# One matrix per chunk in the RWKV-7 chain, the sample's squares at rows 12 and 22, and the dense work in another order

## The chip, the core and the metric

The program runs on one NeuronCore of a Trainium2 chip. The metric is the device time of one execution in microseconds (us), taken as the median of several executions. TensorE (PE) does the matrix products, VectorE (DVE), ScalarE (ACT) and GpSimd (POOL) the elementwise work, and SyncE (SP) issues all the DMAs.

## What is computed

Two layers of a hybrid decoder for a prompt of 512 tokens and a sample group of 8 times 4 tokens (544 columns in all). Layer 0 is windowed attention, layer 1 is RWKV-7 time mixing; both also attend to 256 memory tokens. The change is almost wholly in layer 1, whose core is this recurrence over a state S of 64x64 for each of 12 heads:

```python
def step(S, inp):
    r_t, w_t, k_t, v_t, a_t, b_t = inp
    sa = jnp.einsum('bhvk,bhk->bhv', S, a_t)
    S = S * w_t[:, :, None, :] + sa[..., None] * b_t[:, :, None, :] + v_t[..., None] * k_t[:, :, None, :]
    return S, jnp.einsum('bhvk,bhk->bhv', S, r_t)
...
p = xn @ w_in                                  # 29 column tiles of 128: r, k, v, LoRA, memory query, gate
y = group_norm(y) + sum(r * k * r_k) * v
h = concat([y, o_mem]) * silu(gate)
return h @ w_out
```

## The kernel before

**Layout.** Activations stand as features on partitions and tokens along the free axis. Dense products with weights are split in a high and a low part (`mm1`, L309): three matmuls of 128x128 by 272 or 256 columns (fp32r) for each tile of 128 inputs. Everything else on PE is fp32 and stands in the trace as two records for each matmul that the code issues: the 32 matmuls of a round of 64x64 blocks are 64 records.

**The chunked recurrence.** The 512 prompt tokens are 8 chunks of 64. The 12 heads are three groups g of four heads (two pairs j, each with two heads h). For each pair `decay`, `keys`, `receptance`, `values` and `scores` (L1224 to L1396) prepare the chunk products: `SA` holds the masked scores against a, `SR` those against r, `UV` values and a by token, `BK` the keys by token, and `st.DF` the decay over each whole chunk. `products(g)` (L1400) inverts a 64x64 triangle for each chunk and head: 30 steps of two dependent DVE operations over PSUM (L1444 and L1446), then two rounds of 32x32 products (X, L1460 and L1469). In the steps s = 5 and s = 12 it also squares the sample's small matrix (`square`, L1427). Then come three rounds of 64x64 products: w (L1480, into `AR`), q (the scores times the values) and v (the inverse times q, both L1495), q and v in place in `UV[:, 0]`.

**The chain.** `recur(g)` (L1615) goes through the 8 chunks. In each chunk PE multiplies the state by w (z, four matmuls), DVE adds u (L1670), PE multiplies by the keys (z again, four or eight matmuls), DVE adds the decayed state (L1688), which POOL made (Sd, L1672). The outputs y are products put between these steps (`y_of`, L1635), normalised in `norm` after 4 chunks (`YB`; group 2 in portions of 4, 2 and 2). The next group's inversion cannot begin before `end{g}`: T, the inversion's PSUM tile, and z, the chain's, share one buffer of two banks ("zs"). All groups thus follow one another: inversion, products, chain, inversion, ...

**The order of the work.** `Flow` (L172) is a small planner written by hand: streams (generators) yield a cost and a latency, and the one with the lowest rank that is ready is emitted next; dense streams (`dense` with the column products, `gates`, `outer`) fill in between by a debt rule (`RHO`, `DEBT`). `LAT` are the planned latencies, `RANK` the ranks. The instruction order that results is then ordered on each engine by the framework's own list scheduler; at run time every engine works strictly in that order.

**Around the end.** `gates` (L1736) makes 8 gate columns in the order `GORDER`, the first `GEARLY` without waiting for the last column. They go to DRAM (`ud`). `outer` (L1809) then reads them back (`gated`, L1749: DMA, DVE, ACT, POOL for each of six tiles), into `h1`, which takes the memory of the projections' input `xg` and so cannot be written before the last gate's matmuls. The output projection ("o1", six of eight input tiles, 288 matmuls) follows, and `last` (L1769) for each half of the tokens: the last two tiles (4 and 5) once group 2's norm is done, then the norm and the residual.

**Layer 0.** The sample's cached keys and values come through a ring of `CCB` tiles of 512 KB (`cc`, L654); `sample_values` (L847) reads nine of them for each half of the sample.

Of the kernel before, what the change touches and what calls it, by code (L numbers as in the profile page):

```python
# [24 lines left out]
GORDER = (6, 7, 0, 1, 2, 3, 4, 5)  # L25
# [203 lines left out]
def _device(tc, I, O):  # L229
# [853 lines left out]
    ind2 = rw.tile([128, 2], F32, name="ind2")  # L1083
    hv = rw.tile([128, 4, 6], F32, name="hv")
# [139 lines left out]
    def decay(p):  # L1224
# [30 lines left out]
        for h, r in enumerate(H2):  # L1255
            nc.gpsimd.tensor_copy(st.DF[r, h ^ j], R_[r, 63:512:64])
# [60 lines left out]
    def scores(p):  # L1317
# [74 lines left out]
        yield from by_token((AR.rearrange("p j x t -> p (j x t)"), 2 * j * NT), (q.xv, 0), lambda x: UV[:, x, j], st.UVs[:, j], "av")  # L1392
# [5 lines left out]
    Q0, Q1 = [slice(64 * hh, 64 * hh + 32) for hh in range(2)], [slice(64 * hh + 32, 64 * hh + 64) for hh in range(2)]  # L1398

    def products(g):  # L1400
# [40 lines left out]
        for s in range(1, 31):  # L1441
# [31 lines left out]
        yield f"tokens{2 * g + 1}"  # L1473
        for e in range(2):
            pt = ps_t(f"w{g}{e}")
            for j in range(2):
                for i in range(4):
                    for c, h in block(i, j, e):
                        a = (4 * j + i) * 64
                        nc.tensor.matmul(pt[H2[h], a:a + 64], UV[unit(c, j, h)[0], 0, j, unit(c, j, h)[1]],  # L1480
                                         SA[unit(c, j, h)[0], 0, j, score(c, j, h)[1]], start=True, stop=True)
            both[e](AR[:, :, 0, 0:512].rearrange("p j (i e t) -> p j i e t", e=2, t=64)[:, :, :, e],
                    pt.rearrange("p (j i t) -> p j i t", j=2, t=64))
            yield 1.0, 0

        u = st.u = UV[:, 0].rearrange("p j (c e v) -> p (j c) e v", c=4, e=2)
        for k in range(2):
            for i in range(2):
                pt = ps_t(f"{'qv'[k]}{g}{i}")
                for c in range(4 * i, 4 * i + 4):  # L1490
                    for j, h in PAIRS:
                        r, cs = score(c, j, h)
                        e = turned(c, j, h)
                        a = (c % 4 * 2 + e) * 64
                        nc.tensor.matmul(pt[r, a:a + 64], SA[r, 1 - k, j, cs],  # L1495
                                         u[r, c, e] if k else UV[r, 1, j, unit(c, j, h)[1]], start=True, stop=True)
                both[i](UV[:, 0, i], pt)
                yield 1.0, 0
# [116 lines left out]
    def recur(g):  # L1615

        st = sts[g]
# [3 lines left out]
        AR, BK, SR, UV, DF, u = st.AR, st.BK, st.SR, st.UV, st.DF, st.u  # L1621
        St = rw.tile([128, 2, 64], F32, tag="St", bufs=4, name=f"St{g}i")
        nc.vector.memset(St, 0.0)
        zs = ps_zs(f"z{g}").rearrange("p (e k c v) -> p e k c v", k=2, c=4, v=64)
        yps = None

        states, last = [], None

        def put(out, lhs, rhs, start, stop):
            nc.tensor.matmul(out, lhs, rhs, start=start, stop=stop)  # L1630
            if last:
                tc.add_manual_dep(flow.last(), last.name, SYNC, reason="one half of a bank")
            tc.stamp_issue_order_token(flow.last(), f"chain{g}")

        def y_of(cs, e):  # L1635


            nonlocal yps
            a, b = [ab for ab in YB[g] if ab[0] <= cs[0] < ab[1]][0]
            if cs[0] == a and e:  # L1640
                yps = ps_c("y", f"y{g}_{a}")
            steps = [(c, k, t) for c in cs for k in range(3) for t in range(2) if (c or k) and (k == 0 and t) == e]
            for step in steps:
                c, k, t = step
                for j, h in PAIRS:
                    if turned(c, j, h) == t:
                        r, s = score(c, j, h)
                        lhs = SR[r, 2 - k, j, s] if k else AR[H2[h], j, 1, CH[c]]
                        rhs = (UV[r, 1, j, unit(c, j, h)[1]] if k == 1 else u[r, c, t] if k else states[c][H2[h], j ^ h])
                        y = ((c - a) * 2 + h) * 64  # L1650
                        put(yps[r, y:y + 64], lhs, rhs, e and step == steps[0], not e and step == steps[-1])
            c = cs[1]
            if e:
                return
            if c == b - 1:
                def out(pt):
                    pt = pt[:, 0:(b - a) * 128].rearrange("p (c j t) -> p c j t", j=2, t=64)
                    for j in range(2):
                        add_affine(2 * g + j, pt[:, :, j], slice(64 * a, 64 * b), True)
# [149 lines left out]
    def outer():  # L1809
        for e in ("gates", "end1", "norm1_8", "norm1s"):  # L1810
            yield e
# [125 lines left out]
```

## Time and profile before

| | |
|---|---|
| median of 3 runs | 826.03 us (824.16 to 829.28) |
| the profiled execution | 825.58 us, of which its span is 823.8 us |
| mean granted TensorE clock | 0.956 of full speed |
| PE busy | 759.0 us (92%) |
| DVE busy | 457.7 us (56%) |
| POOL busy | 353.0 us (43%) |
| ACT busy | 339.4 us (41%) |

The span is what the profile shows; 1.8 us of the execution lie around it. A busy PE is not PE at its peak: a matmul's end is modelled, and at the lower granted clock (1.2 in place of 2.4 GHz) the same work is busy for twice as long. The product of busy time and granted clock of a stretch is therefore used below as the work that was done in it.

### The profile page before, as it was taken

Reading aid. Unit: us, or ns where it says so; the run is one execution under the profiler, and the core shown is the slowest. Engines: PE = TensorE matmul, PEld = TensorE weight load, DVE = VectorE, ACT = ScalarE, POOL = GpSimd, SP = SyncE. Lnnn points to the kernel's source line nnn. Section 1 sums busy time; section 2 is a strip of 40 time slices with the busy share of each in tenths; the row PEclk is TensorE's granted clock in tenths of the full one; section 3 lists DMA queues with packets and bytes.
Section 4 is the critical chain, followed back from the end, with each engine's and each line's share of the span. In section 5 each row is a group of like instructions: output and inputs, shape, how many; then the busy total and the mean of one; then the engine's idle time right before and its main releaser. Section 6 shows DMA issues by size and latency. Waiting matters only on the chain. (4 is left out here: it accounts for less than half of the span.)

```text
span 823.8 us, 20121 instructions
## 1 busy us (share of the span) xinstructions
PE 759.0 (92%) x8278; PEld 645.8 (78%) x8278; DVE 457.7 (56%) x1094; ACT 339.4 (41%) x780; POOL 353.0 (43%) x389
## 2 busy tenths in 40 slices
PE   6899999999987988999999999999979999699974
PEld 5777878878974776688988889898868888489963
DVE  7724312265468246663454579745887437752465
ACT  7434521133344235535886246522454233222221
POOL 4643213322220244864542346643556335543454
PEclk9999999999999998999999999999979999689987
DMA  7462745773213656225222432211202313423012
GB/s 242 138 226 66 201 146 204 260 271 131 80 53 115 225 174 223 87 96 184 64 66 91 150 136 84 76 39 56 79 31 80 106 54 110 155 81 92 15 47 99
DMA packets 59089, 99.51 MB, mean 121 GB/s; under 512 B 6416, under 2 KB 24112, under 8 KB 58960
## 3 DMA queue, kind: packets, MB, share of 16 engines
q1 hardware_dynamic: 58996, 98.22, 36.6%
q8 instruction: 65, 1.06, 0.5%
q14 instruction: 28, 0.22, 0.1%
HBM read 84.15 MB, written 14.05 MB: 119 GB/s over the span
## 5 line engine op out<-in xcount | busy, mean ns | idle before, releaser
L303 POOL TENSOR_TENSOR lo_b<-raw_b,hi_b 128x512 fp32r<-128x512 f32 x58 | 79.0, 1363 | 111.0 <-ACT hi_b L302 88.2
L303 POOL TENSOR_TENSOR lo_a<-raw_a,hi_a 128x512 fp32r<-128x512 f32 x44 | 57.2, 1300 | 147.9 <-ACT hi_a L302 132.3
L302 ACT CAST hi_b<-raw_b 128x512 fp32r<-128x512 f32 x58 | 36.2, 625 | 39.6 <-PE b_h L312 12.5
L302 ACT CAST hi_a<-raw_a 128x512 fp32r<-128x512 f32 x44 | 27.3, 619 | 59.8 <-DMA raw_a<-in_w_in_a 10.2
L310 PE MATMUL b_h<-xg,hi_b 128*128 128x272 f32 x160 | 47.9, 306 | 1.7 <-DVE xv L1127 1.4
L311 PE MATMUL b_h<-xg,lo_b 128*128 128x272 f32 x160 | 47.7, 303 | 0.0
L312 PE MATMUL b_h<-xg,hi_b 128*128 128x272 f32 x160 | 47.1, 300 | 0.0
L310 PEld LDWEIGHTS b_h<-xg,hi_b 128*128 128x128 f32 x160 | 31.0, 196 | 3.5 <-DVE xv L1127 1.5
L1444 DVE TENSOR_TENSOR TX<-T,TT 128x30 f32<-128x30 f32 (+14 forms) x90 | 29.4, 326 | 5.3 <-ACT T L1418 3.4
L311 PEld LDWEIGHTS b_h<-xg,lo_b 128*128 128x128 f32 x160 | 31.3, 197 | 1.3 <-issue 1.0
L312 PEld LDWEIGHTS b_h<-xg,hi_b 128*128 128x128 f32 x160 | 31.2, 197 | 0.3 <-issue 0.2
L1446 DVE TENSOR_TENSOR T<-T,TX 128x30 f32<-128x30 f32 (+14 forms) x90 | 30.1, 334 | 2.1
L310 PE MATMUL o<-h,hi_o1a 128*128 128x256 f32 (+1 forms) x64 | 20.0, 325 | 4.3 <-ACT h L1757 4.3
L1672 POOL TENSOR_TENSOR Sd<-St,DF 128x128 f32<-128x128 f32 x21 | 8.5, 404 | 34.1 <-DVE St L1688 26.9
L312 PE MATMUL o<-h,hi_o1a 128*128 128x256 f32 (+1 forms) x64 | 19.7, 323 | 0.5 <-POOL h L1758 0.3
L764 ACT COPY PT<-pa 128x512 f32<-128x512 f32 x16 | 9.3, 582 | 26.2 <-issue 15.2
L311 PE MATMUL o<-h,lo_o1a 128*128 128x256 f32 (+1 forms) x64 | 19.5, 317 | 0.0
L748 ACT ACTIVATE P<-P,m 128x768 f32<-128x768 f32 x16 | 14.9, 934 | 11.1 <-DVE m L747 11.1
L1367 PE MATMUL sc<-AR,BK 64*64 64x128 f32 x384 | 18.4, 277 | 0.0
L763 PE MATMUL pa<-ident,P 128*128 128x128 f32 x96 | 14.3, 278 | 3.7 <-DVE P L750 1.4
L310 PEld LDWEIGHTS o<-h,hi_o1a 128*128 128x128 f32 x64 | 13.0, 211 | 5.7 <-ACT h L1757 5.6
L1758 POOL TENSOR_TENSOR h<-ug,h 128x544 fp32r<-128x544 f32 (+2 forms) x10 | 11.1, 1119 | 12.7 <-ACT h L1757 12.7
(1056 smaller groups left out, 2835.4 us busy)
## 6 DMA issues: line engine op xcount, KB each, us to landing
raw_b<-in_w_in_b SPq DMA_DIRECT2D x58, 256.0 KB, 2.7
raw_a<-in_w_in_a SPq DMA_DIRECT2D x44, 256.0 KB, 2.7
kc<-in_kc SPq DMA_DIRECT2D x18, 512.0 KB, 4.9
vc<-in_vc SPq DMA_DIRECT2D x18, 512.0 KB, 4.8
out_win<-t SPq DMA_DIRECT2D x12, 272.0 KB, 2.4
PB<-bd SPq DMA_DIRECT2D x4, 576.0 KB, 8.6
x<-in_x SPq DMA_DIRECT2D x8, 272.0 KB, 5.5
xr<-in_x SPq DMA_DIRECT2D x16, 136.0 KB, 4.0
```

Of the source, the lines that this page charges most:

```text
L302: nc.scalar.copy(hi, raw)
L303: lo_eng.tensor_tensor(lo, raw, hi.bitcast(F32), ALU.subtract)
L310: nc.tensor.matmul(ps[:, :n], hi, xh, start=first, stop=False)
L311: nc.tensor.matmul(ps[:, :n], lo, xh, start=False, stop=False)
L312: nc.tensor.matmul(ps[:, :n], hi, xl, start=False, stop=last)
L748: nc.scalar.activation(P, P, AF.Exp, bias=m1[:, 0:1], scale=1.0, accum_out=m1[:, 1:2])
L763: nc.tensor.transpose(dst, P[:, j * 128:j * 128 + 128], ident)
L764: nc.scalar.copy(PT[hh][:, 0:4, :], pa4.rearrange("p (j q) -> p j q", j=4))
L1367: nc.tensor.matmul(pts[e][unit(c, j, h)[0], a:a + 128], BK[H2[h], j, x, CH[c]], AR[H2[h], j, :, CH[c]], start=True, stop=True)
L1444: nc.vector.tensor_tensor(pd, TP[:, 0:s, s:s + 1].to_broadcast([128, s, w]), TT[:, s:s + 1, s + 1:32].to_broadcast([128, s, w]), ALU.mult)
L1446: nc.vector.tensor_tensor(TP[:, 0:s, s + 1:32], TP[:, 0:s, s + 1:32], pd, ALU.add)
L1758: nc.gpsimd.tensor_tensor(out.h1[:, 1, j, ts], uj, out.h1[:, 0, j, ts].bitcast(F32), ALU.subtract)
```

## The change

The chain is rewritten so that each chunk's state follows from the last by one matrix, S(c+1) = M(c) S(c) + N(c). M(c), 64x64 for each head, is the keys times w plus the diagonal of the decay; N(c) are the keys times the two value terms. In the same way r is replaced by r plus a product with w. M, N and the new r are made for all chunks ahead of the chain, so that each chunk has one round trip PE, DVE, PE in place of two. A new stream `queries(g)` does the round q beside the inversion and makes the diagonal on POOL; `products` then does one round of 32 matmuls over 128 columns (w and v together) in place of w, q and v. The squares move to rows 12 and 22. `outer` starts when the gates are done and waits for the norms of groups 0 and 1 only before its fifth tile (after 6, 7, 0, 1). The planner's constants change, the portions of group 2's norm become 4 and 4, and the ring of layer 0 grows from 5 to 8 tiles. `LOD` is empty, so the line in `gated` that names it stays on POOL.

```diff
-GORDER = (6, 7, 0, 1, 2, 3, 4, 5)
+GORDER = (6, 2, 3, 0, 5, 7, 4, 1)
-GEARLY = 4
-LAT = [4.0, 5.82, 0.4, 0.6, 5.42, 5.2, 1.5, 0.94, 2.61, 0.6, 1.2]
-RANK = [4, 2, 7, 3, 2, 4, 6, 9]
-RHO, DEBT = 0.35, 0.5
+GEARLY = 5
+LAT = [4.0, 5.82, 0.23, 0.71, 6.5, 5.2, 1.5, 1.32, 1.69, 0.3, 1.2]
+RANK = [5, 2, 7, 3, 3, 3, 7, 9]
+RHO, DEBT = 0.42, 0.338
+LOD = ()
-CCB = 5
+CCB = 8
-YB = (((0, 4), (4, 8)),) * 2 + (((0, 4), (4, 6), (6, 8)),)
+YB = (((0, 4), (4, 8)),) * 3
...
+    id2 = rw.tile([128, 64], F32, name="id2")
+    for r in (slice(0, 64), slice(64, 128)):
+        nc.gpsimd.tensor_copy(id2[r], ident[r, r])
...
-        for h, r in enumerate(H2):
-            nc.gpsimd.tensor_copy(st.DF[r, h ^ j], R_[r, 63:512:64])
+        for k in range(2):
+            nc.gpsimd.tensor_copy(st.DF[:, j ^ k, k::2], R_[:, 64 * k + 63:512:128])
...
+    def queries(g):
+        yield f"scores{2 * g + 1}"
+        yield f"tokens{2 * g + 1}"
+        st = sts[g]
+        for j in range(2):
+            pt = ps_t(f"q{g}{j}")
+            for i in range(4):
+                for h in range(2):
+                    for c in (2 * i + j, (2 * i + j + 1) % 8):
+                        r, a = unit(c, j, h)
+                        nc.tensor.matmul(pt[r, a], st.SA[r, 1, j, score(c, j, h)[1]], st.AR[r, j, 0, a], start=True, stop=True)
+            nc.scalar.copy(st.UV[:, 1, j], pt)
+            yield 0.85, 0
+        M = st.M = st.SA[:, 1].rearrange("p r (c t) -> p r c t", t=64)
+        nc.gpsimd.tensor_tensor(M, id2[:, None, None, :].to_broadcast([128, 2, 8, 64]),
+                                st.DF[:, :, :, None].to_broadcast([128, 2, 8, 64]), ALU.mult)
+        flow.done(f"queries{g}", 1.0)
...
-            if s in (5, 12):
+            if s in (12, 22):
                 yield 0.0, LAT[9]
-                square(s // 12)
+                square(s // 22)
...
+        yield f"queries{g}"
+        for j in range(2):
             for i in range(2):
+                pt = ps_t(f"w{g}{j}{i}").rearrange("p (x a) -> p x a", x=2)
                 for c in range(4 * i, 4 * i + 4):
+                    c = (c + j) % 8
+                    for h in range(2):
+                        r, a = unit(c, j, h)
+                        nc.tensor.matmul(pt[r, :, a.start - 256 * i:a.stop - 256 * i], SA[r, 0, j, score(c, j, h)[1]],
+                                         UV[r, :, j, a], start=True, stop=True)
+                both[i](UV[:, :, j, 256 * i:256 * i + 256], pt)
+                yield 0.9, 0
...
+        pts = with_W("M", lambda c, j, h: BK[unit(c, j, h)[0], j, 0, unit(c, j, h)[1]])
+        for r in range(2):
+            m = M[:, r, 1:8].rearrange("p c t -> p (c t)")
+            nc.vector.tensor_tensor(m, m, pts[r][:, 64:512], ALU.add)
+        yield 1.3, 0
+        zs = ps_zs(f"z{g}").rearrange("p (r a) -> p r a", r=2)
         for c in range(8):
             for k in (1, 0):
                 for j, h in PAIRS:
+                    r, a = unit(c, j, h)
+                    put(zs[H2[h], (c + j) % 2, CS[c]], BK[r, j, k, a], AR[r, j, 0, a] if k else UV[r, 1, j, a],
+                        k == 1, k == 0)
...
+        for r in range(2):
+            nc.scalar.copy(rest[:, r], zs[:, r])
...
+        pts = with_W("R", lambda c, j, h: SR[unit(c, j, h)[0], 0, j, score(c, j, h)[1]])
...
+        y_of(0, range(4), (1, 2), 0)
+        yield 1.6, 0
+        for c in range(1, 8):
+            if c == 7:
+                y_of(1, range(4, 8), (0,), 0)
+            for j, h in PAIRS:
+                put(zs[H2[h], c, j ^ c % 2], M[H2[h], (c + j) % 2, c], states[c][H2[h], j ^ (c - 1) % 2], True, True)
+            state(c)
+            step = flow.last(ET.DVE)
+            yield 0.2, 0
...
+            if c == 5:
+                y_of(0, range(1, 4), (0,), 1)
+                finish(0)
+                yield 0.3, 0
+            if c == 6:
+                y_of(1, range(4, 8), (1, 2), 0)
+                yield 1.6, 0
+            yield 0.0, LAT[3]
+        y_of(1, range(4, 8), (0,), 1, step)
+        finish(1)
...
     def outer():
-        for e in ("gates", "end1", "norm1_8", "norm1s"):
-            yield e
+        yield "gates"
         out.h1 = pxg.tile([128, 2, 8, NT], F32R, tag="xg", name="h1")
         for j in (6, 7, 0, 1, 2, 3):
+            if j == 2:
+                for e in ("end1", "norm1_8", "norm1s"):
+                    yield e
             gated(j)
```

`with_W` issues 28 matmuls of 64x64 (chunks 1 to 7, four heads) into two banks; `state(c)` is one DVE add of 128x128 from PSUM to a new state tile; `finish(b)` calls `norm`. The new r needs four DVE adds over a half of the chunks each.

## Rows read from the trace of the kernel before

**Rows 1.** Page, parts 1 and 2: busy time, and the granted clock in 40 slices.
```profile
PE 759.0 (92%) x8278; PEld 645.8 (78%) x8278; DVE 457.7 (56%) x1094; ACT 339.4 (41%) x780; POOL 353.0 (43%) x389
PEclk9999999999999998999999999999979999689987
```
**Rows 2.** Windows: length, busy us (count) of PE, PEld, DVE, ACT, POOL, PEclk, DMA.
```profile
240.00:272.00 32.00, 23.37 (x243) 15.42 (x242) 25.06 (x56) 15.23 (x33) 1.67 (x2) 0.95 0.25 83
...
480.00:599.00 119.00, 118.04 (x1661) 107.10 (x1659) 84.90 (x231) 55.48 (x132) 59.78 (x65) 0.99 0.23 69
599.00:609.00 10.00, 4.01 (x37) 3.39 (x36) 8.97 (x26) 7.21 (x17) 7.08 (x11) 0.64 0.15 52
609.00:700.00 91.00, 89.10 (x1365) 79.84 (x1366) 57.70 (x139) 30.80 (x63) 44.29 (x45) 0.96 0.25 79
700.00:730.00 30.00, 20.25 (x124) 15.86 (x124) 23.64 (x64) 7.69 (x16) 13.38 (x12) 0.66 0.42 130
730.00:790.00 60.00, 58.81 (x1034) 52.73 (x1034) 23.40 (x54) 15.67 (x35) 26.39 (x30) 1.00 0.22 64
790.00:823.80 33.80, 18.40 (x149) 16.08 (x144) 20.04 (x52) 7.14 (x18) 18.42 (x24) 0.75 0.22 72
```
**Rows 3.** Line L1444, the three inversions: ns min/median/max, first and last start.
```profile
L1444 DVE TENSOR_TENSOR TX<-T,TT x30: 189/344/407, 480.9 to 515.9; 128x30 f32<-128x30 f32 x2, 128x58 f32<-128x58 f32 x2, 128x84 f32<-128x84 f32 x2, 128x108 f32<-128x108 f32 x2
...
L1444 DVE TENSOR_TENSOR TX<-T,TT x30: 189/349/403, 583.2 to 620.9; 128x30 f32<-128x30 f32 x2, 128x58 f32<-128x58 f32 x2, 128x84 f32<-128x84 f32 x2, 128x108 f32<-128x108 f32 x2
...
L1444 DVE TENSOR_TENSOR TX<-T,TT x30: 189/350/406, 690.8 to 727.4; 128x30 f32<-128x30 f32 x2, 128x58 f32<-128x58 f32 x2, 128x84 f32<-128x84 f32 x2, 128x108 f32<-128x108 f32 x2
```
**Rows 4.** Line L1688, the three chains' state additions: ns, first and last start.
```profile
L1688 DVE TENSOR_TENSOR St<-z,Sd x7: 276/282/291, 552.1 to 581.3; 128x128 f32<-128x128 f32 x7
...
L1688 DVE TENSOR_TENSOR St<-z,Sd x7: 278/290/292, 658.6 to 688.8; 128x128 f32<-128x128 f32 x7
...
L1688 DVE TENSOR_TENSOR St<-z,Sd x7: 280/291/293, 756.3 to 787.0; 128x128 f32<-128x128 f32 x7
```
**Rows 5.** The chain that ended last, group 2's products and chain: start, us, what.
```profile
742.82 1.83 PE w L1480 x58
...
745.98 2.01 PE q L1495 x64
...
749.19 2.01 PE v L1495 x64
...
752.22 0.33 PE o L311
752.55 0.13 PE o L312
...
754.27 0.28 PE z L1630 x8
```
**Rows 6.** Timeline of PE: 64x64 blocks over 128 and 512 columns (start, us).
```profile
525.93 1.09 PE L1367 MATMUL sc<-AR,BK 64*64 64x128 f32 x28
...
780.36 1.03 PE L1593 MATMUL sts<-UX,BKs 64*64 64x512 f32 x4
```
**Rows 7.** Groups by line and shape: busy us, mean ns, idle before and releasers.
```profile
L1389 POOL TENSOR_TENSOR BK<-BK,DT 128x512 f32<-128x512 f32 x12 | 12.3, 1045 | 1.4 <-PE sc L1367 1.4
...
L1758 POOL TENSOR_TENSOR h<-ug,h 128x544 fp32r<-128x544 f32 x6 | 8.1, 1345 | 10.0 <-ACT h L1757 10.0
...
L1594 DVE TENSOR_TENSOR S0s<-sts,S0s 128x512 f32<-128x512 f32 x6 | 4.1, 686 | 1.2 <-PE sts L1593 1.2
```
**Rows 8.** Timeline of SP's queue and of PE around the cached values of layer 0.
```profile
260.05 1.59 SPq L853 DMA_DIRECT2D vc<-in_vc  x3
...
267.75 3.35 PE L856 MATMUL so<-vc,sP 128*32 128x256 f32 x32 [4.29 <-DMA vc<-in_vc]
```
**Rows 9.** Timeline of PE: a square of group 1, and the end of the output projection.
```profile
601.70 0.40 PE L1431 MATMUL n<-SAs,TX 32*32 32x32 f32 x8 [1.80 <-DVE bv L1552]
...
782.65 0.29 PE L312 MATMUL o<-h,hi_o1a 128*128 128x288 f32 x1
...
799.20 0.84 PE L310 MATMUL o<-h,w2h 128*128 128x288 f32 x2
```

More of the change, by code (lines that the diff above doesn't have):

```diff
@@ L1635, in y_of @@
[L1635 to L1644, printed above, removed]
-                for j, h in PAIRS:
[L1646 to L1659, printed above, removed]
-                norm(g, yps, 2 * (b - a), f"_{b}", out)
@@ new lines, in recur, with put, with_W @@
+        CS = [slice(64 * c, 64 * c + 64) for c in range(8)]
+        def put(out, lhs, rhs, start, stop, after=None):
+            nc.tensor.matmul(out, lhs, rhs, start=start, stop=stop)
+            if after:
+                tc.add_manual_dep(flow.last(), after.name, SYNC, reason="one half of a bank")
+            by_turns(f"chain{g}")
+        def with_W(name, rhs):
+            pts = [ps_t(f"{name}{g}{r}") for r in range(2)]
+            for c in range(1, 8):
+                for j, h in PAIRS:
+                    r, a = unit(c, j, h)
+                    put(pts[(c + j) % 2][H2[h], CS[c]], UV[r, 0, j, a], rhs(c, j, h), True, True)
+            return pts
@@ L1684, in recur @@
-                    put(zs[H2[h], e, 1, c % 2], BK[r, j, k, cs], UV[r, 1, j, cs] if k else u[r, c, e], k == 1, k == 0)
-            Sn = rw.tile([128, 2, 64], F32, tag="St", bufs=4, name=f"St{n}")
-            sn = zs[:, ::-1, 1, c % 2] if c % 2 else zs[:, :, 1, c % 2]
-            if c:
-                nc.vector.tensor_tensor(Sn, sn, Sd, ALU.add)
-            else:
-                nc.vector.tensor_copy(Sn, sn)
-            step = flow.last(mybir.EngineType.DVE)
-            yield 0.5, LAT[3]
@@ new lines, in recur, with y_of @@
+        pts = with_W("R", lambda c, j, h: SR[unit(c, j, h)[0], 0, j, score(c, j, h)[1]])
+        for r in range(2):
+            for k in range(2):
+                cs = slice(2 - k, 8, 2)
+                x = AR[:, r ^ k, 1, 0:512].rearrange("p (c t) -> p c t", t=64)[:, cs]
+                nc.vector.tensor_tensor(x, x, pts[r].rearrange("p (c t) -> p c t", t=64)[:, cs], ALU.add)
+        yield 1.3, 0
+        def y_of(b, cs, ks, t, after=None):
+            a, e = YB[g][b]
+            first = b not in yps
+            if first:
+                yps[b] = ps_c("y", f"y{g}_{a}")
+            for c in cs:
+                for k in ks:
+                    for n, (j, h) in enumerate(PAIRS):
+                        if k or (c and turned(c, j, h) == t):
+                            r, s_ = score(c, j, h)
+                            v = unit(c, j, h)[1]
+                            lhs = SR[r, 2 - k, j, s_] if k else AR[H2[h], j, 1, CH[c]]
+                            rhs = AR[r, j, 0, v] if k == 1 else UV[r, 1, j, v] if k else states[c][H2[h], j ^ (c - 1) % 2]
+                            y = ((c - a) * 2 + h) * 64
+                            put(yps[b][r, y:y + 64], lhs, rhs, first and c == cs[0] and k == ks[0] and n < 2, bool(t) and c == cs[-1],
+                                after)
@@ new lines, in finish, with out @@
+        def finish(b):
+            a, e = YB[g][b]
+            def out(pt):
+                pt = pt[:, 0:(e - a) * 128].rearrange("p (c j t) -> p c j t", j=2, t=64)
+                for j in range(2):
+                    add_affine(2 * g + j, pt[:, :, j], slice(64 * a, 64 * e), True)
+            norm(g, yps[b], 2 * (e - a), f"_{e}", out)
+        y_of(0, range(4), (1, 2), 0)
+        yield 1.6, 0
+        for c in range(1, 8):
+            if c == 7:
[5 more added lines that the diff above has]
+            yield 0.2, 0
+            if c == 3:
+                y_of(0, range(1, 4), (0,), 0)
+                yield 0.3, 0
+            if c == 5:
+                y_of(0, range(1, 4), (0,), 1)
+                finish(0)
+                yield 0.3, 0
+            if c == 6:
+                y_of(1, range(4, 8), (1, 2), 0)
+                yield 1.6, 0
+            yield 0.0, LAT[3]
@@ L1731, in dense @@
             if p % 2:
+                flow.spawn(RANK[3], queries(g))
                 flow.spawn(RANK[3], products(g))
@@ L1757, in gated @@
         nc.scalar.copy(out.h1[:, 0, j, ts], uj)
[L1758 removed]
+        (nc.vector if j in LOD else nc.gpsimd).tensor_tensor(out.h1[:, 1, j, ts], uj, out.h1[:, 0, j, ts].bitcast(F32), ALU.subtract)
     def by_row(i, tag, width, name):
```

74 lines of the change are left out of this document (17 added, 57 removed).

## The prediction

> **What bounds the kernel now.** I read the page's first two parts first: PE is busy for 759.0 of 823.8 us, no other engine for more than 457.7, and the granted clock is full except in some slices, most of them in the last third [rows 1]. Then the windows by stage [rows 2], the three inversions [rows 3], the three chains [rows 4], and last single bursts on PE [rows 5, 6]. The reader should see two limits lying almost on one another.
>
> The first is a path. Inversion 0 runs from 480.9 to about 516, 1 from 583.2 to 621, 2 from 690.8 to 728 [rows 3]; the last state of chain 0 is added at 581.3, of chain 1 at 688.8, of chain 2 at 787.0 [rows 4]. Each inversion starts 2 us after the chain ahead of it. So from 481 to 790 the groups stand end to end, some 100 us each: 40 of inversion, 25 of products, 35 of chain. Within a chain six steps take 29.2, 30.2 and 30.7 us, 5.0 us a step [rows 4].
>
> The second is PE itself, which fills the waits of that path with dense columns. Work, as busy time times granted clock, is 116.9, 2.6, 85.5, 13.4 and 58.8 us in the five windows from 480 to 790, in all 277 of 310 us [rows 2]. Only 33 us are open: 2.1, 7.4, 5.5, 16.6 and 1.2 us. A shorter path can give back no more than these, less what the change adds on PE. That decides the size of my number.
>
> **Products.** Removed: w and v on the path, and q between them, 64 records each, which are 32 matmuls of 64x64 by 64 columns: 2.0 us a round, 31 ns a record [rows 5]. From the first w to the end of v it takes 8.4 us (742.82 to 751.20) [rows 5]. Afterwards q stands in `queries`, beside the inversion, and one round remains, 32 matmuls over 128 columns that lie in only two of the four 64x64 tiles. No row shows that form. Below it is bounded by 2.2 us: scores over 128 columns, in four tiles, take 1.09 us for 28 records, so no more than 39 ns each [rows 6]. Above it is bounded by twice a v, 4.0 us. Four records over 512 columns in two tiles take 1.03 us, 0.26 us a record, or 64 ns for 128 columns [rows 6], 4.1 us for 64 of them; but the end of the burst is counted in so few records. I take 3.4 us, nearer to this row because it is the one with two tiles. With a copy out of PSUM of 0.7 us (a 128x512 DVE operation on PSUM) [rows 7] the path keeps about 4.4 us: 4 us a group are saved, 12 in all. PE does 3.4 in place of 4.0 us, 0.6 less a group.
>
> The Trainium skill's TensorEngine Tiling (Array Packing), in Instruction Overhead, gives every matmul a fixed cost of about 60 cycles, so that few columns cost what 60 do. Taken with it that time then goes with the columns, an estimate from that page is that 128 columns cost twice 64, the 4.0 us of the upper bound, and the sum below would be 2 us higher. The trace disagrees for the scores, whose 128 columns take no more than 39 ns a record beside 31 for 64 [rows 5, 6].
>
> POOL makes the diagonal M over 128x1024: two of the 1.05 us products of 128x512 [rows 7], 2.1 us a group. It lies under the inversion's 38 us [rows 3]; without that cover w would wait for it, since `products` yields for `queries`, and behind it on POOL stand the low halves of the weights. Seven Sd a group leave POOL. The two copies for id2 and the other DF pattern are as short as what they replace; decay and layer 0's end hide them.
>
> **Chain.** Removed: one of two round trips a step. Added on PE: M, 28 matmuls, and R, 28, at 63 ns each: 3.5 us a group. N and y keep their 64 and 92. The new path: M 1.8, R 1.8, N 4.0, the first y 2.0 us, 152 matmuls, 9.6 us; around them two DVE adds and a copy at up to 0.7 each [rows 7], of which about 1.9 us show; the other y, 60 matmuls, 3.8 us; and seven steps. A step is at least z's 0.28 on PE and 0.29 on DVE [rows 4, 5], 0.57 us. Where six dense matmuls (0.125 each) come between it is 1.5 us: the return to dense costs 0.33 in place of 0.13 us for the first matmul [rows 5]. Seven steps take 4 to 10.6 us. In all 19 to 26, I take 24 us, nearer the end with dense work in every step, since PE is full. Before it was 7 times 5.0 and the last y, 37 us. Saved: 13 a group (11 to 18), 39 in all. Behind each step's matmuls PE's whole order waits for DVE, and DVE's order holds norm operations of 0.7 us [rows 7]; that is a rival below. The last y's wait for the last state has only the end of its own group behind it.
>
> **Sum on the path and on PE.** The path could give 51 us (42 to 66). PE has 33 open and gets 3 times (3.5 - 0.6), 9 us (5 to 11): it can give 24 at most. So PE becomes the bound, and what counts is which open stretches close.
> - 599 to 609, 7.4 us open: PE waits in its order, 1.80 us of it for a square [rows 9], which the change moves to a later row. Another order may hold another such wait; 3 us stay.
> - 700 to 730, 16.6 us open at clock 0.66 [rows 2]: the last gate must be through before h1 can be written, then six tiles go through DMA, DVE, ACT and POOL, 1.35 us each on POOL [rows 7], with two buffers. The change takes away waits that were not the late ones there. What it gives is other PE work for this stretch: with a shorter path more of group 2's products fall into it, and one gate fewer stands behind the columns. I keep 9 us.
> - The other 8.8 us are spread; 6 stay.
>
> That is 18 of 33: 15 us closed, 9 added, 6 saved.
>
> **The tail.** The output projection ends at 782.65, but the second half's last products begin only at 799.20 [rows 9], because the chain is not through before 787 [rows 4]. With the chain done earlier the first half's 48 matmuls (6 us) and some 3 us of its sums remain between: 9 in place of 16.5 us, 7 saved (nothing, if the chain still ends last; then the norm of four chunks at once adds 2 us). The 24.6 us from there to the end stay.
>
> **Layer 0.** Three loads of cached values are issued at 260.05, when the first tiles of the ring come free, and PE waits 4.29 us for them; the burst behind runs at a lower clock [rows 8], with 0.95 granted over the window [rows 2]. Eight tiles let them go ahead of that; the ninth still waits. I count 5 us (0 to 6: what follows may be bound by its own loads). Gate order, ranks and planned latencies cost nothing themselves; they choose where dense work stands, so the open stretches above are their price.
>
> The sum, against the profiled execution's 825.6 us (its span and 1.8 us around it, 0.5 below the median shown): 825.6 - 6 - 7 - 5 = 807.6; I say 807.
>
> **The rivals.**
> - *All open time closes* (the path falls so far ahead that PE never waits before the tail): 6 of 33 us stay, 27 closed, 9 added: 825.6 - 18 - 7 - 5 = 796, call it 795. For it speaks that the path gives twice what PE can use; against it the h1 stretch, which no path shortens.
> - *The planner gives it back*: no open stretch closes, and the 9 us on PE are paid in full; with the ring's 5 and a third of the tail it is 825.6 + 9 - 5 - 3 = 827. For it: inversion 1 starts when PE has just made its scores, inversion 2 too, so dense work in front of the scores can hold the path back just as before. Against: in a shorter path it has less reason to.
> - *PE waits in its own chain* (the other side): 21 steps and some 12 handovers for M, N, R and y stand in PE's order at planned gaps of 0.7 us; where DVE has a norm or an evacuation or two in front, PE stands still, dense work behind it included. At 1.0 us each, 33 places cost 33 us on top of my sum: 840. Above 0.83 us a place it decides for slower. Against it: 21 z waits of that kind now show hardly any idle PE (1.2 open us over group 2's chain [rows 2]).
>
> **How the numbers follow.** My case 0.58 (797 to 818), all closed 0.14 (788 to 802), given back 0.18 (818 to 834), waits 0.10. A measurement of this kernel can tell about 1% from no change, 817.8 to 834.3 us. Faster: 0.56 + 0.14 + 0.02 of the third = 0.72; within: 0.18; slower: 0.10. The range goes from 790 to 828: nearly all of my case, most of the first rival and half of the second, some 8 in 10.
>
> **What would show it.** Right: state additions one per chunk at 1 to 2 us distance (L1688's were 5.0); the chain of group 2 over before the output projection ends; PE's work from 480 up by about 9 us; the wait for vc gone at 260; a new w burst of 3 to 4 us. Wrong: holes of 5 us and more on PE at the clock's lower level before the last inversion; PE idle on the state additions; w far from 3.4 us; an inversion that starts late because its scores are late. Most at risk is the split of the 33 open us, where I chose and did not read.

## The result, and the profile after

The changed kernel takes 822.8 us against 827.8 (medians of 20 executions each): ratio 0.9931, interval 0.991 to 0.9952. The forecast was 807. The profiled execution of after has a span of 821.6 us (823.4 with what lies around it), that of before 823.8 (825.6): 2.2 us apart, so of the 5 us between the medians 2.8 are where each profiled execution stands to its own median.

Page of after, busy time and granted clock in 40 slices, as in [rows 1]; PE is busier by 7.6 us:
```profile
PE 766.6 (93%) x8422; PEld 653.1 (79%) x8422; DVE 463.0 (56%) x1078; ACT 342.9 (42%) x788; POOL 350.6 (43%) x372
...
PEclk9999998999999999999999999899999999779986
```
Windows of after, columns as in [rows 2]:
```profile
240.00:272.00 32.00, 27.26 (x362) 18.91 (x354) 26.71 (x58) 16.35 (x35) 2.85 (x2) 1.00 0.33 118
...
480.00:599.00 119.00, 114.12 (x1622) 102.80 (x1620) 85.69 (x211) 56.21 (x130) 59.51 (x62) 0.97 0.20 63
599.00:609.00 10.00, 10.00 (x150) 8.98 (x150) 8.92 (x27) 4.64 (x12) 4.66 (x5) 1.00 0.24 77
609.00:700.00 91.00, 88.42 (x1375) 79.75 (x1373) 57.53 (x138) 32.83 (x71) 43.32 (x40) 1.00 0.26 83
700.00:730.00 30.00, 23.32 (x198) 18.75 (x196) 25.76 (x68) 9.41 (x20) 16.58 (x14) 0.72 0.48 145
730.00:790.00 60.00, 58.68 (x1052) 53.35 (x1051) 25.09 (x54) 15.97 (x35) 23.82 (x23) 1.00 0.22 64
790.00:821.60 31.60, 16.95 (x99) 15.13 (x97) 17.33 (x43) 6.44 (x16) 16.64 (x22) 0.69 0.23 77
```
PE's work from 480 to 790 us, busy time times granted clock, is 110.7 + 10.0 + 88.4 + 16.8 + 58.7 = 284.6 us in place of 277.1 [rows 2]. Open are 25.4 us in place of 32.9. So 7.5 us closed, and by 790 PE has done 7.5 us more: work that the change adds, and work that moved in from either side. Over the whole trace, with each busy stretch weighted by its granted clock, PE's work is 734 us in before and 744 in after.

The three inversions of after (ns, first and last start), the last state of its three chains, then the prompt's scores of pairs 3 and 5, from which inversions 1 and 2 are made, in before and in after:
```profile
L1468 DVE TENSOR_TENSOR TX<-T,TT x30: 190/349/407, 476.8 to 508.9; 128x30 f32<-128x30 f32 x2, 128x58 f32<-128x58 f32 x2, 128x84 f32<-128x84 f32 x2, 128x108 f32<-128x108 f32 x2
L1468 DVE TENSOR_TENSOR TX<-T,TT x30: 189/338/408, 585.9 to 622.3; 128x30 f32<-128x30 f32 x2, 128x58 f32<-128x58 f32 x2, 128x84 f32<-128x84 f32 x2, 128x108 f32<-128x108 f32 x2
L1468 DVE TENSOR_TENSOR TX<-T,TT x30: 190/349/407, 695.7 to 727.7; 128x30 f32<-128x30 f32 x2, 128x58 f32<-128x58 f32 x2, 128x84 f32<-128x84 f32 x2, 128x108 f32<-128x108 f32 x2
```
```profile
L1676 DVE TENSOR_TENSOR St<-z,BK x1: 283/283/283, 566.3 to 566.3; 64x128 f32<-64x128 f32 x1
...
L1676 DVE TENSOR_TENSOR St<-z,BK x1: 275/275/275, 680.0 to 680.0; 64x128 f32<-64x128 f32 x1
...
L1676 DVE TENSOR_TENSOR St<-z,BK x1: 278/278/278, 773.3 to 773.3; 64x128 f32<-64x128 f32 x1
```
```profile
L1367 PE MATMUL sc<-AR,BK x64: 269/269/321, 569.5 to 576.5; 64*64 64x128 f32 x64
...
L1367 PE MATMUL sc<-AR,BK x64: 269/269/320, 674.5 to 684.7; 64*64 64x128 f32 x64
```
```profile
L1371 PE MATMUL sc<-AR,BK x64: 269/269/320, 570.2 to 579.8; 64*64 64x128 f32 x64
...
L1371 PE MATMUL sc<-AR,BK x64: 269/269/321, 679.1 to 688.6; 64*64 64x128 f32 x64
```
The chains end 15, 9 and 14 us earlier than in before [rows 4]. But inversions 1 and 2 gain nothing of it: in these two profiles they start 2.7 and 4.9 us *later* [rows 3], and in e15, which keeps after's order up to 700 us, at 582.0 and 691.4, 1.2 us earlier than in before and 0.6 later. Before they followed the chain by 2 us, now by 19.6 and 15.7. They wait for the scores, whose last records start 3.3 and 3.9 us later in after: in both kernels an inversion starts 6 to 7 us behind them. What the chain gave, the order did not pass on.

Before had hardly any room at these two places. TT, the scores turned for the inversion, was complete (its last operation on DVE) 0.9 and 0.6 us before the chain's last state let ACT copy it to T:
```profile
580.59 0.09 DVE L1413 MEMSET TT<- 128x32 f32 x1
...
581.59 0.59 ACT L1418 COPY T<-TT 128x512 f32<-128x512 f32 x1 [1.48 <-DVE St L1688]
...
688.45 0.09 DVE L1413 MEMSET TT<- 128x32 f32 x1
...
689.15 0.59 ACT L1418 COPY T<-TT 128x512 f32<-128x512 f32 x1 [1.70 <-DVE St L1688]
```
A chain that ends earlier, with the scores where they stood, could bring these inversions forward by no more than that.

By stage, in the profiled executions, against before: layer 1's first column starts 2.7 us earlier (349.1, before 351.8), inversion 0 4.1 us earlier, the last gate matmul 1.3 us earlier (699.4, before 700.7), the last matmul of the output projection 0.4 us later (783.1, before 782.65), the second half's last products 4.3 us earlier (794.9, before 799.2), and the kernel ends 2.2 us earlier.

### The profile page after: what moved, and what is told of

Read it like the earlier page. It is cut to its first block, busy times and chain, and to the rows that moved or that the text cites. A ratio compares the mean times of both kernels' runs of the same rounds, so it can differ in the third digit from the quotient of the medians.

```text
span 821.6 us, 20338 instructions
## 1 busy us (share of the span) xinstructions
PE 766.6 (93%) x8422; PEld 653.1 (79%) x8422; DVE 463.0 (56%) x1078; ACT 342.9 (42%) x788; POOL 350.6 (43%) x372
## 4 chain that ended last, share of the span: by engine, by line
PE 74%; DVE 14%; DMA 4%; issue 3%; ACT 2%; POOL 1%; SPq 1%; DVEq 0%; POOLq 0%; ACTq 0%
PE o L311 3%; PE o L312 2%; PE o L313 2%; PE y L1637 2%; PE b_h L311 2%; PE b_h L312 2%; PE sc L1371 2%; PE b_h L313 2%; PE Sx L558 2%; PE z L1637 1%; PE w L1505 1%; PE o L772 1%; PE ox L582 1%; PE pa L764 1%; DMA ug<-ud 1%
## 5 line engine op out<-in xcount | busy, mean ns | idle before, releaser
L304 POOL TENSOR_TENSOR lo_b<-raw_b,hi_b 128x512 fp32r<-128x512 f32 x58 | 76.8, 1323 | 122.6 <-ACT hi_b L303 79.8
L303 ACT CAST hi_a<-raw_a 128x512 fp32r<-128x512 f32 x44 | 27.3, 620 | 70.9 <-DMA raw_a<-in_w_in_a 15.5
L312 PEld LDWEIGHTS b_h<-xg,lo_b 128*128 128x128 f32 x160 | 30.2, 190 | 0.5
L749 ACT ACTIVATE P<-P,m 128x768 f32<-128x768 f32 x16 | 14.9, 935 | 16.3 <-DVE m L748 16.3
L1393 POOL TENSOR_TENSOR BK<-BK,DT 128x512 f32<-128x512 f32 x12 | 12.7, 1084 | 7.8 <-PE sc L1371 7.8
L764 PEld LDWEIGHTS pa<-ident,P 128*128 128x128 f32 x96 | 10.6, 142 | 6.7 <-issue 2.8
```

Of the source, the lines that this page charges most:

```text
L303: nc.scalar.copy(hi, raw)
L304: lo_eng.tensor_tensor(lo, raw, hi.bitcast(F32), ALU.subtract)
L312: nc.tensor.matmul(ps[:, :n], lo, xh, start=False, stop=False)
L749: nc.scalar.activation(P, P, AF.Exp, bias=m1[:, 0:1], scale=1.0, accum_out=m1[:, 1:2])
L764: nc.tensor.transpose(dst, P[:, j * 128:j * 128 + 128], ident)
```

## Experiments

The answer of a run is its ratio to the kernel before, run beside it; a difference between two runs is that of their ratios, 0.001 being 0.8 us. Work is PE's work from 480 to 790 us, as above. e3, e4, e13 and e14 compute less than the kernel.

| run | what | ratio (interval) | work, us |
|---|---|---|---|
| before | | 1 | 277.1 |
| after | | 0.9931 (0.991 to 0.9952) | 284.6 |
| e1 | rewrite, planner constants of before | 1.0332 (1.0294 to 1.0371) | 255.1 |
| e2 | before, planner constants of after | 1.0071 (1.0046 to 1.0095) | 273.5 |
| e3 | after, 16 us of gate products out | 0.9876 (0.9842 to 0.9911) | 272.1 |
| e4 | before, the same out | 0.9897 (0.9858 to 0.9937) | 264.8 |
| e5 | after, scores ranked first | 1.005 (1.0019 to 1.0082) | 278.2 |
| e6 | after, slower states | 1.0064 (1.003 to 1.0098) | 272.2 |
| e7 | after, six gated buffers | 0.9955 (0.9928 to 0.9983) | 283.4 |
| e8 | after, ring of five | 1.0065 (1.0035 to 1.0096) | 278.4 |
| e9 | before, ring of eight | 0.9911 (0.9885 to 0.9936) | 280.6 |
| e10 | after, ring of seven | 0.9999 (0.9968 to 1.0031) | 280.5 |
| e11 | before, one latency 0.60 to 0.61 | 1.0027 (0.9999 to 1.0054) | 277.7 |
| e12 | after, one latency 0.71 to 0.60 | 1.0056 (1.0027 to 1.0086) | 275.8 |
| e13 | before, one round trip off the chain | 1.0015 (0.9989 to 1.004) | 277.5 |
| e14 | e13 and e4 together | 0.9937 (0.991 to 0.9965) | 263.5 |
| e15 | after, sample's output first | 0.9898 (0.9865 to 0.9931) | 287.7 |
| e16 | e9, sample's output first | 0.9935 (0.9909 to 0.996) | 278.8 |
| e17 | e15, tail opened on DVE | 0.9859 (0.9827 to 0.9891) | 286.6 |
| e18 | e16, tail opened on DVE | 0.99 (0.986 to 0.994) | 278.3 |

**Which part brings the gain: e1, e2, e8, e9, e10.**
```diff
 e1: after with  GORDER, GEARLY, LAT, RANK, RHO, DEBT of before
 e2: before with GORDER, GEARLY, LAT, RANK, RHO, DEBT of after
 e8, e10: after   -CCB = 8   +CCB = 5   (e10: +CCB = 7)
 e9: before       -CCB = 5   +CCB = 8
```


> The rewritten chain and products with the planner constants of before (gate order, early gates, latencies, ranks, the two ratios). Theory P (between 480 and 790 us PE is the bound, and the shorter path only turns into waiting for scores that stand behind dense work): the rewrite alone adds its 7 us of PE work and closes as little open time, 823 to 832 us. Theory S (the new constants hold the scores of pairs 3 and 5 back, 11 and 5 us later than in the kernel before): with the old ones inversions 1 and 2 start 5 to 11 us earlier and the time falls to 810 to 817 us.

> The kernel before with the planner constants of after, its chain and products as they were. If the constants by themselves bring the 5 us that were measured: 820 to 824 us. If they pay only together with the shorter path (theory P: the long chain of before becomes the last to end again): 827 to 840 us.

> The kernel after with the ring for layer 0's cached tiles back at five. The wait for the cached values is 0.9 us in the kernel after and 4.29 in the one before, and layer 1's first column starts 2.7 us earlier in after. If the ring is what brought that, and nothing later takes it back: 2 to 4 us slower, 825 to 827. If later waits take it back: 822 to 824, with layer 1 starting 2.7 us later.

> The kernel before with the ring for layer 0's cached tiles at eight in place of five, nothing else. By the trace of after the ring lets layer 1 start 2.7 us earlier; the kernel after lost 9 us when its ring was put back to five, 2.5 of them before 480 us and the rest behind, where only the order differs. Theory R (the ring itself is worth 9 us): 817 to 820 us. Theory O (2.5 to 3 us are the ring's, the rest is the order that the scheduler happens to write behind it): layer 1 starts 2 to 3 us earlier, and the time is anywhere between 818 and 832, with the difference to that standing in PE's waits behind 480 us.

> The kernel after with a ring of seven in place of eight. It changes the places of 426 of PE's 6100 instructions, the first of them in layer 0's last part. If the ring's size is what counts: between the 822.8 of eight and the 831.8 of five, 823 to 826, and layer 1 starts less than 2 us later. Theory O: layer 1 starts within 2 us, but the time behind it moves by more than that start, up or down, 818 to 832.

The kernel before with the larger ring alone has all of the gain: 0.9911 beside 0.9931. In these runs everything else in the change nets to nothing. Rewrite and constants do not stand alone: the rewrite with the old constants costs 33 us against after, the new constants on the old chain 6 us against before. Windows of e1:
```profile
609.00:700.00 91.00, 80.83 (x1292) 72.42 (x1289) 53.80 (x130) 34.89 (x74) 37.50 (x39) 0.92 0.18 57
...
730.00:790.00 60.00, 47.97 (x781) 41.44 (x781) 24.28 (x53) 14.50 (x28) 21.29 (x20) 0.77 0.28 79
```
In these two alone PE does 74.4 and 36.9 us of work where after does 88.4 and 58.7. Neither theory of e1 had this. Four rows of what PE waits for in e1 from 480 to 790 us (us in total, times, longest):
```profile
PE o L311 <- ACT h L1802: 8.2, 5, 4.0
PE sc L1371 <- DVE bv L1317: 3.6, 1, 3.6
...
PE R L1637 <- issue: 1.8, 1, 1.8
PE y L1637 <- issue: 1.7, 2, 1.3
```
With z's 1.5 us the rewritten chain's own products wait 5.0 us there; the longest waits are for h1, for the operand of a score, and for single operations of DVE and ACT that stand late.

The ring's worth is larger than the wait that it removes. In e8 PE waits 3.15 us for the cached values and layer 1 starts 2.5 us later than in after, yet 11 us are lost; its last gate matmul starts at 705.3, not 699.4. In e9's profile layer 1 starts 1.1 us earlier than in before, and the median falls by 6. e10 starts layer 1 no later than after (348.1) and is 6 us slower. The program's scheduler places instructions by modelled times, and a shift in layer 0 moves what stands behind it too (of PE's 6100 instructions some 1000 in e8, 426 in e10, some 1200 of before's in e9), so "the ring alone" is a ring and a new order; how the 6 us divide is not settled.

**Whether path or work is the limit: e3, e4, e6, e13, e14.**
```diff
 e3, e4 (gate columns only; the two other products stay)
-        nc.tensor.matmul(ps[:, :n], hi, xl, start=False, stop=last)
 e6 (c < 7)
+                nc.vector.tensor_tensor(Sx, zs[:, c], rest[:, :, CS[c]], ALU.add)
+                nc.gpsimd.tensor_copy(S, Sx)
 e13, e14 (Ux: a tile that nothing reads)
-                nc.vector.tensor_tensor(u[:, c], zs[:, :, 0, c % 2], u[:, c], ALU.add)
+                nc.vector.tensor_tensor(Ux, zs[:, :, 0, c % 2], u[:, c], ALU.add)
```


> The kernel after without the third product (high half of the weights by low half of the activations) of the eight gate columns: 128 matmuls of 272 columns at 0.125 us, 16 us of PE work in the stretch from 480 to 700 us left out; everything else stays. Theory P: the time falls by nearly all of it, 12 to 16 us, to 807 to 811. Theory S (the path with its late scores is the bound, PE only fills it): it falls by 0 to 6 us, to 817 to 823.

> The kernel before without the third product of the eight gate columns, the same 16 us of PE work left out. If its path (inversion, products, chain end to end) was the limit: the time falls by 0 to 6 us, to 822 to 828. If PE was: by 12 to 16, to 812 to 816. Both theories of after take the path as the limit here, with PE close behind it: 3 to 8 us, 820 to 825.

> The kernel after with six of the seven state additions of each chain written to another tile and copied by POOL to their place, so that each step is 0.4 to 0.6 us longer, 8 to 11 us over the three chains. Theory P (the path has slack: 19.6 us behind chain 0, 15.7 behind chain 1, and chain 2 ends before the output projection): chains 2.5 to 4 us longer each, time up by 0 to 3 us, to 820 to 826. Theory S (path is the bound): up by 8 to 11 us, 830 to 834. Theory O: PE waits 0.4 to 0.6 us at each step behind which its order stands, also 5 to 10 us up, but with the idle time written against the chain's matmuls and with inversions 1 and 2 starting no later.

> The kernel before with the first of the two round trips of each chain step taken off the path: the DVE addition of z into u goes to a spare tile that nothing reads, so that the state products wait no longer for it (the correction of u is left out of the result). Every matmul stays, and PE's instructions stand in the same order; DVE's change place at 21. Theory P (work on PE sets the time, the chain's waits are covered by dense columns): the same as before within 3 us, 825 to 829. Theory S (the path of inversion, products and chain sets it): 21 round trips of 0.8 to 2 us less, 17 to 40 us off the path, and the time falls by 6 us at least, to 795 to 821.

> As the run before, and the third product of the eight gate columns left out as well: 16 us less PE work and the shorter path together. e4 took out the work alone and fell by 7.4 us. Theory P with the path close behind (each limit holds when the other is moved alone): both together bring more than the sum of the two, 12 to 18 us, 810 to 816. Theory S: the time is that of the run before, less 0 to 3 us. If neither counts and only the order does: within 3 us of e4, 818 to 824.

e13 is the plainest of all runs: PE's instructions stand in the same order as in before. Its state additions, group by group:
```profile
L1688 DVE TENSOR_TENSOR St<-z,Sd x7: 274/281/292, 553.2 to 582.3; 128x128 f32<-128x128 f32 x7
...
L1688 DVE TENSOR_TENSOR St<-z,Sd x7: 280/292/292, 659.8 to 690.0; 128x128 f32<-128x128 f32 x7
...
L1688 DVE TENSOR_TENSOR St<-z,Sd x7: 280/292/293, 757.3 to 788.0; 128x128 f32<-128x128 f32 x7
```
29.1, 30.2 and 30.7 us for six steps, as in [rows 4], though one of the two round trips is gone. What PE waits for the removed addition is one row in the waits of before, and one in those of e13:
```profile
PE z L1630 <- DVE UV L1670: 0.6, 1, 0.6
```
```profile
PE z L1630 <- DVE Ux L1670: 0.6, 1, 0.6
```
A step of 5.0 us was never two round trips: it is the dense matmuls that the order puts between them. With the order untouched the removed round trip is worth nothing. What a shorter path is worth when the order is written anew, e13 does not say; after is one such order.

Nor is PE's work the limit of the whole kernel. Of the 16 us taken out, the times fell by 5 us in e3 and 8.5 in e4. Up to the output projection the work counts in full: its last matmul starts 18 us earlier in e3 (765.0, after 783.1) and 24 in e4 (758.9, before 782.65); counted from layer 1's start it is 19, 22 and, in e14, 21 us, more than the 16 since other work moved behind it. But the first half's last products start only 11 us earlier (772.1, after 783.2; 770.1, before 781.3): they need group 2's norms, and so its chain. The open time of the fixed windows, which grows by 12.5 us to 37.9 in e3 and by 12.3 to 45.2 in e4, is in part this tail, which 790 already cuts into. And e14, with PE's order exactly that of e4, is no faster than e4: the two do not add up to more. Neither theory holds alone: theory S does not hold in e13, theory P not at the end of e3 and e4. What is left is the order in which PE's instructions stand, for path and dense work at once. That is argued, not isolated: in e3, e4 and e6 some 660, 820 and 640 of PE's instructions stand elsewhere as well, so each of them is an edit and a new order.

e6, with 8 to 11 us more latency in the chains, lost 11 us: not in a later inversion 2 (693.3, after 695.7), but behind it, where PE did 12.6 us of work from 700 to 730 instead of 16.8, waiting 10.6 us in all for the high halves of h1 (after: 3.9).

**What the order is worth: e5, e11, e12.**
```diff
 e5: after   -RANK = [5, 2, 7, 3, 3, 3, 7, 9]   +RANK = [5, 2, 0, 3, 3, 3, 7, 9]
 e11: before LAT[3] 0.6 to 0.61;  e12: after LAT[3] 0.71 to 0.60
```


> The kernel after with the rank of the scores at 0 in place of 7, so that the planner never puts dense columns in front of them; nothing else is changed. Theory S (late scores hold the path, and the path the time): the masks of pairs 3 and 5 come 5 to 12 us earlier than 592.5 and 693.9, inversions 1 and 2 as much, and the time falls to 810 to 818 us. Theory P (PE is full, a path ahead of it buys nothing): the inversions start earlier, the time stays within 3 us, 820 to 826. Theory O (what counts is only whether PE's written order meets its operands; a new order made with the same latencies stalls elsewhere): inversions earlier or not, PE idle between 480 and 700 grows from 7 to 12 us and more, time 827 to 845.

> The kernel before with one planned latency (between two states) at 0.61 in place of 0.60. No instruction is added or left out; 196 of PE's 6028 and 82 of DVE's 1096 stand elsewhere, from about 480 us on. If the work on PE and on the path sets the time: 826 to 829, as before. Theory O (whether PE's order meets its operands sets it): off by 2 us or more, up or down, with the open time of the windows behind 480 us changed by as much.

> The kernel after with the planned latency between two states at 0.60 in place of 0.71. Same work; 1449 of PE's 6100 instructions stand elsewhere, from about 530 us on. If the work on PE and on the path sets the time: 821 to 825. Theory O: off by 4 us or more, more likely up (824 to 835), with the open time behind 530 us changed by as much and the start of inversions 1 and 2 moved by several us.

In e5 the last scores of pair 3 start 4.0 us earlier (575.8), but now chain 0 ends 21 us later (587.2) and inversion 1 starts behind it, at 589.4. Those of pair 5 start 25 us later (713.6), inversion 2 starts at 719.6, and the kernel loses 10 us. In e12 no instruction is added, 1449 of PE's stand elsewhere, and it loses 10 us too (windows of e12):
```profile
609.00:700.00 91.00, 86.18 (x1376) 74.97 (x1376) 59.88 (x144) 31.87 (x67) 40.46 (x39) 0.95 0.26 82
700.00:730.00 30.00, 22.12 (x210) 18.16 (x210) 23.80 (x54) 9.08 (x19) 15.55 (x15) 0.73 0.41 124
730.00:790.00 60.00, 58.24 (x936) 52.59 (x931) 20.99 (x45) 15.05 (x32) 24.53 (x20) 0.94 0.24 72
```
Its inversion 2 starts 7 us earlier than in after (688.7) and its last chain ends 5 us earlier, but the last gate matmul starts 11 us later (710.5), and everything behind it. Before's nudge (e11) moved less and cost 0 to 0.5%. Over the kernels made from after that keep its work, the time follows the work done by 790: 6.4, 6.2, 8.8, 4.1 and 1.2 us less in e5, e8, e12, e10 and e7, for 10, 11, 10, 6 and 2 us of time, and 3.1 more in e15 for 3 us less. That locates the loss ahead of the tail; it does not name its cause.

**The stretch behind the gates and the tail: e7, e15, e16, e17, e18.**
```diff
 e7
-            us[j] = rw.tile([128, NT], F32, tag="u", bufs=2, name=f"ug{j}")
+            us[j] = tmp(f"ug{j}")
 e15, e16 (sample; both are the two halves of its old body)
+        for f in (outs, states) if g == 2 else (states, outs):
+            yield from f()
 e17, e18 (the first half's scaling by rp waits for the second half's last z addition)
+                if not i:
+                    tc.add_manual_dep(flow.last(ET.DVE), out.added.name, SYNC, ...)
```


> The kernel after with the gated activations of the output projection loaded into the six temporary tiles instead of the two gate tiles; nothing else is changed. If the two tiles hold up the stretch from 700 to 730 us (each load waits until POOL has read the tile before): the loads start together at 700, PE's open time there falls from 13 to 5 to 8 us, the time to 815 to 819. If DVE's order holds it up (inversion 2 stands between the gating products): open time stays at 11 to 13 us, the time at 820 to 824.

> The kernel after with the sample's output products and their norm ahead of its state products, in the last group only; 74 of PE's 6100 instructions stand elsewhere, all behind 700 us. In after the second half's last products wait for that norm (its last addition at 793.4 us, the first products at 794.9), not for the chain, which ended at 773.6. If that is what is late in the tail: those products start at 791 to 792, 3 to 4 us earlier, and the time falls by 2 to 4 us, to 819 to 821. If DVE's queue (the closing operations of the first half stand in front of the second half's additions) is late instead: they start earlier, but PE waits the longer for DVE behind them, and the time is 822 to 824.

> The kernel before with the ring at eight and with the same move of the sample's output products in the last group; 122 of PE's 6028 instructions stand elsewhere, all behind 700 us. In the kernel before the chain of the last group ends at 787 us (783.3 in its profile with the ring at eight) and its norm holds the second half's products, not the sample. So no gain from the move: 820 to 824, as with the ring alone. If the sample's norm was as late as the chain's: 817 to 820.

> The kernel of e15 with the closing operations of the first half of the output tied behind the last addition of the second half on DVE. In e15 PE waits 2.98 us there at 799.0 us, behind eight such operations; PE's order stays, five DVE instructions change place. If that wait is on the way to the end: the last products end 2 to 4 us earlier and the time falls by 2 to 3 us from 819.7, to 816 to 818. If the first half's operations, done later, then stand in front of the second half's on DVE and POOL: 819 to 821.

> The kernel of e16 (before, ring of eight, sample first) with the same tie. Its chain of the last group ends at 783 us and its norm is through at about 793, so the second half's products cannot start before 794. Theory T (the short chain is worth something only here, in the tail): it falls by 0 to 3 us to 819 to 822, and stays 3 to 5 us behind e17. If the rewrite has no worth at all: within 1 us of e17. If its added PE work costs more than the tail gives: faster than e17.

e7 closed 4 us from 700 to 730 (20.7 us of work, after 16.8) and gave 6.5 back from 730 to 790 (52.2, after 58.7): no gain. The tail is where the short chain may pay. Timeline of after, DVE and PE: the norm of the sample, and the second half's first products:
```profile
793.44 0.41 DVE L1562 SCALAR_TENSOR_TENSOR bv<-gn2s,pv,bv 128x32 f32<-128x32 f32 x2
```
```profile
794.93 0.53 PE L311 MATMUL o<-h,w2h 128*128 128x288 f32 x2
...
800.15 0.61 PE L311 MATMUL o<-h,w2h 128*128 128x288 f32 x1 [2.04 <-DVE z L1835]
```
Timeline of e15, and of e17:
```profile
788.61 0.37 PE L311 MATMUL o<-h,w2h 128*128 128x288 f32 x1
...
799.00 0.61 PE L311 MATMUL o<-h,w2h 128*128 128x288 f32 x1 [2.98 <-DVE z L1841]
```
```profile
791.25 0.37 PE L311 MATMUL o<-h,w2h 128*128 128x288 f32 x1
...
799.15 0.29 PE L313 MATMUL o<-h,w2h 128*128 128x288 f32 x1
```
Counted from the last gate matmul, so that what went before drops out, the second half starts 95.5 us later in after, 93.5 in e15 and 92.9 in e17, and the kernel ends 122.2, 120.6 and 118.4 us later. e17's wait is gone (its last product starts 7.9 us after its first). It is 0.7% faster than after by the ratios (0.9859 beside 0.9931; the intervals just part) and the fastest of all. In e16 the same move brings nothing, as expected: there the chain is late. With ring, sample and tail alike, the rewrite (e17, 818.3 us) stands 3 us ahead of the old chain (e18, 821.4); the intervals overlap, so this worth is likely, not shown.

## Why the prediction was wrong, step by step

- **Two limits, path and PE.** The step that failed. I read three groups standing end to end, each inversion 2 us behind the chain, as a path with a price per step that gives 51 us, so that PE becomes the bound and open time closes. (The parts named add to 45 to 66 us, not 42 to 66.) What stood there was an order: the chain was as long as the dense work put into it (e13: one round trip less, six steps still 29 to 31 us, the time within 0.4%), and the inversions start 6 to 7 us behind their scores, which in before were complete only 0.9 and 0.6 us ahead of the chain. So chains that end 15 and 9 us earlier left the start of inversions 1 and 2 where it was, or later. The 822.8 lies in the stated range only because that was drawn to take in half of the second rival.
- **The split of the 33 open us.** 18 forecast to stay, 25.4 stayed. 599 to 609 closed wholly (3 forecast); 700 to 730 kept 13.2 (9); the rest, 8.8 us, did not shrink to 6 but grew to 12.2, 8.3 of it from 480 to 599. There inversion 0 holds DVE busy for 8.4 to 9.9 of every 10 us from 480 to 520, PE waits in its order, and the clock fell to 0.66 from 520 to 530. e15, with the same order up to 700, kept 1.00 in that slice: 3 us of it belong to the execution.
- **PE's added work**: 9 forecast; about 7 by the bursts (10 by the whole trace). M and R were cheaper than the 3.5 us a group (2.4 to 2.5 of busy time), the one w burst dearer than my 3.4: two halves of 2.0 us and more (timeline of after),
```profile
740.00 2.23 PE L1505 MATMUL w<-UV,SA 64*64 64x128 f32 x32
...
744.00 2.01 PE L1505 MATMUL w<-UV,SA 64*64 64x128 f32 x32
```
63 ns a record, twice the 31 of [rows 5]. That is the upper bound, and what the estimate from the Trainium skill's TensorEngine Tiling (Array Packing), in Instruction Overhead, gave; the trace agrees with it here, and I should have taken it. It is 0.6 us a group and more, so the one round in place of two saved PE nothing.
- **The chain, 13 us a group**: the shortening came. From M to the last state it took 22, 29 and 25.5 us, 24 forecast, though the steps were longer than the 1 to 2 us of my sign: six took 14.5, 18.1 and 16.3 us. It bought waiting, the second rival (*the planner gives it back*, 827), whose "dense work in front of the scores" is what the rows show; 7.5 open us did close, which that rival had not.
- **The tail, 7 us**: 2.6 came. From the last matmul of the output projection to the second half's it took 11.8 us in place of 16.5 (9 forecast), and from there to the end 26.7 in place of 24.6, which I had held fixed. The chain was over in time, as forecast; what I overlooked is that the second half waits for the sample's norm as well, which was late next, and behind it for DVE's closing operations. From the last gate to the end only 0.9 us are left of the 2.6.
- **The ring, 5 us**: from 240 to 272 us PE did 27.3 us of work in place of 22.2 [rows 2], and 2.7 of these 5 us were left at layer 1's start; 6 by e9's median, a new order included. Right in size, and as large as the whole gain.
- **The earlier start of the gated tiles** costs and brings nothing: with the old waits put back every engine's instructions are the same, in the same order. POOL's diagonal M took 1.9 us, 2.1 forecast, under cover.
- **The third rival** (*PE waits in its own chain*, 0.10) did not come: from 480 to 790 PE waits 4.2 us at y and z in after, and in e1, which lost the 33 us, 5.0 at R, y and z. I treated the planner's constants as choosing among open stretches; they were worth 33 us to the rewrite.

## What to carry over

A chain that takes as long as the dense work written between its steps is not a path: before pricing its round trips, look at the rows between two steps and at PE's waits for them; if those are under a microsecond, a shorter chain saves nothing until the order is written anew. Look also at the other input of the stage behind the chain: here the scores were ready less than a microsecond before it. Where a planner writes one order for all streams, every edit ahead of it draws a new order worth some 10 us here, so measure each part of a change alone, its smallest part first, and judge a stage from its own window. Ask of every stage that waits for several events which one is late *next*.

## What the runs showed of the chip

With one and the same program the time goes with the mean granted clock of the execution: the 20 executions of after go from 816.7 us at 0.974 to 825.8 at 0.958. A single profile is one draw of these, so stages of two profiles a few us apart can't be told apart by their ends alone. Of 64x64 blocks, a record over 128 columns took 63 ns where two of the four tiles are filled (w), and no more than 39 where four are (the scores, [rows 6]); over 64 columns it took 31 ns in two tiles (v, [rows 5]) and 19 to 24 in four (M and R, 56 records in 1.04 to 1.36 us).
